# One 512-column product for both parts of x where the weights are stationary, and a later place for scores and transposes in an encoder kernel

## The chip, the cores and the metric

The kernel runs on one core of one Trainium2 chip. The metric is the device time of one execution in microseconds. The traces come from the hardware profiler, one execution each. The engines are named as in the profile: PE (TensorE; PEld are its weight loads), DVE (VectorE), ACT (ScalarE), POOL (GpSimd) and SP (SyncE, which issues the loads).

## The reference

A two-layer encoder over 256 tokens of width 1024. Each layer is a gated feed-forward block, a mixer block and a second feed-forward block, each followed by a layer norm:

```python
for l in range(2):
    x = layer_norm(ALPHA * x + 0.5 * (silu(x @ wg1[l]) * (x @ wu1[l])) @ wd1[l])      # d_ff = 2816
    u, gb, gc, h, q, k, v = jnp.split(x @ w_in[l], [256, 512, 768, 1024, 1536, 2048], axis=-1)
    y_a = pool_mixer(u)                          # window means minus the token, a small product
    y_b = gb * conv3(gc * h)                     # depthwise, width 3
    y_c = neighbourhood_attention(q, k, v)       # 8 heads of 64, 4 x 64 grid, bias, softmax
    x = layer_norm(ALPHA * x + jnp.concatenate([y_a, y_b, y_c], -1) @ w_out[l])
    x = layer_norm(ALPHA * x + 0.5 * (silu(x @ wg2[l]) * (x @ wu2[l])) @ wd2[l])
```

All of it is in fp32. The kernel gets fp32 accuracy from the faster fp32r format: x and the weights are each split into a high part (hi, the value rounded to fp32r) and a low part (lo, the rest), and a product is hi·hi + hi·lo + lo·hi.

## The kernel before

**Weights.** They are loaded in units of 128 x 1024 values on SP's queue. ACT makes the high part of a unit (`upper`, L218, `whi`), DVE the low part (`lower`, L223, `wlo`). 11 pairs are kept ahead.

**Three forms of product.** `x_stat` (L345 to L347) holds a tile of x and streams 512 columns of weights; `r_stat` (L370 to L372) does the same for the down and output products. `w_stat` (L349) is the other way round: a 128 x 128 chunk of weights is stationary and the 256 tokens of x stream, so that the result comes out with features on the partitions. It is used where that layout is wanted: for the last 256 columns of gate and up in each feed-forward block, and in the mixer for q0, k0, q1, k1, gc and h, 256 columns each: 20 products in all. A product has two column tiles of 128 (`ft`), each the sum over 8 chunks of three matmuls: high weights by high x (L358), high weights by low x (L359), low weights by high x (L360). Both column tiles go side by side into one PSUM bank, which one consumer reads as 512 columns.

**Order.** The order on each engine is that in which the code emits it, steered by a paced clock (`Pacer`). `pc.step(us)` moves that clock on by the PE time of the work just emitted; `pc.at(delay, tag, fn)` puts a piece of work off until the clock has passed now plus delay; `pc.need(tag)` emits what is still put off. Steps also emit the splits of the weights that have landed. A step is a quarter of a w_stat product, so what is put off comes out at quarters.

**The mixer.** v, u and gb come first. Then `qk(0)` makes q0 and k0 for the first four heads and puts off their attention, two heads (a pair, `first` and `second`) at a time; `qk(1)` does it for the other four; then come gc and h. Attention of a pair has four pieces: `scores` (PE L799, DVE's bias and maximum L808 and L810, ACT's exponentials L813), `normalise` (DVE L823 and L825), `transposed` (PE L834, ACT's copies `PT` L839) and `weighted` (PE L848, then yT by ACT L861 and DVE L862). The delays are A_S and A_STEP for the scores, then A_NORM, A_TR and A_PV from piece to piece. `conv_mixer` (L771) is a chain on DVE from z = gc·h (L894) over the taps (L775, L777) to the product with gb (L778), then ACT's cast (L780) and DVE's rest (L781). At the end the output product runs over eight chunks, first those of y_a, then of attention, then of the convolution.

**Banks.** PSUM has eight banks. Four ("acc") hold the long sums and the scores, four ("mm") rotate among all other products and transposes; a new one takes the bank that was released first, and PE waits until its last reader is through.

The x parts are two tiles (`xhi`, `xlo`), each written once per block by `transpose_x` (L319).

Of the kernel before, what the change touches and what calls it, by code (L numbers as in the profile page):

```python
# [9 lines left out]
F32 = mybir.dt.float32  # L10
F32R = mybir.dt.float32r
AF = mybir.ActivationFunctionType
ALU = mybir.AluOpType
# [3 lines left out]
P = 128  # L17
SEQ = 256
NT = SEQ // P
D = 1024  # L20
KC = D // P
# [3 lines left out]
HD = 64  # L25
# [8 lines left out]
QB = GRID // 2  # L34
# [17 lines left out]
H_TR = 4.1  # L52
U_TR = 2.6
POOL_AT = 22.0
A_S = 1.5
A_STEP = 0.8
A_NORM = 3.6
A_TR = 2.2
A_PV = 1.4
BIAS_AT = A_S + A_STEP + A_NORM + A_TR + 0.6  # L60

# [1 line left out]
LOWER = 0.9  # L63

MM512 = 0.218
MM256 = 0.1095


class Pacer:
# [75 lines left out]
def encoder_kernel(  # L145
# [7 lines left out]
    PE, ACT, DVE, POOL, SP = nc.tensor, nc.scalar, nc.vector, nc.gpsimd, nc.sync  # L153
# [5 lines left out]
    xp = ctx.enter_context(tc.tile_pool(name="xp", bufs=1))  # L159
    tp = ctx.enter_context(tc.tile_pool(name="tp", bufs=5))  # L160
# [9 lines left out]
    def nm(s):  # L170
        counter[0] += 1
        return f"{s}_{counter[0]}"

    def f32(t):
        return t.bitcast(F32)
# [4 lines left out]
    def mirrored(v):  # L180

        dims = [list(d) for d in v.ap]
        step, n = dims[-1]
        dims[-1] = [-step, n]
        return bass.AP(tensor=v.tensor, offset=v.offset + (n - 1) * step, ap=dims)
# [4 lines left out]
    def bank(tag="mm"):  # L190
        pool = ps_mm if tag == "mm" else ps_acc
        return pool.tile([P, 512], F32, tag=tag, name=nm(tag))
# [66 lines left out]
    def behind(q):  # L259

        return [[4 * q - 4, 4 * q - 3], [4 * q - 2, 4 * q - 1]]
# [20 lines left out]
    pc = Pacer(units, fetch, upper, lower)  # L282
# [29 lines left out]
    POOL.memset(half_t, -0.5)  # L312

    def new_xT():
        hi = xp.tile([P, KC, SEQ], F32R, tag="xhi", name=nm("xhi"))
        lo = xp.tile([P, KC, SEQ], F32R, tag="xlo", name=nm("xlo"))
        return hi, lo

    def transpose_x(t, k0, n, xT, tag="mm"):  # L319
        ts = slice(t * P, (t + 1) * P)  # L320
# [25 lines left out]
            PE.matmul(ps, xT[1][:, kc, ts], hi[:, j, :], start=False, stop=False)  # L346
            PE.matmul(ps, xT[0][:, kc, ts], lo[:, j, :], start=False, stop=(kc == KC - 1))  # L347

    def w_stat(ps, key, xT):  # L349

        for ft in range(2):
            c = slice(ft * P, (ft + 1) * P)
            for i in range(2):
                hi, lo = pc.get((*key, i))
                for j in range(4):
                    kc = i * 4 + j
                    o = ps[:, ft * SEQ : (ft + 1) * SEQ]
                    PE.matmul(o, hi[:, j, c], xT[0][:, kc, :], start=(kc == 0), stop=False)  # L358
                    PE.matmul(o, hi[:, j, c], xT[1][:, kc, :], start=False, stop=False)  # L359
                    PE.matmul(o, lo[:, j, c], xT[0][:, kc, :], start=False, stop=(kc == KC - 1))  # L360
                if ft == 1:
                    pc.free((*key, i))
                if ft == 0 or i == 0:
                    pc.step(12 * MM256)

    def r_stat(ps, key, act, t, n, first, last, c=slice(0, 512), again=False):

# [33 lines left out]
    def finish(keys, act, acc, last_key, next_gb, store, stop):  # L401

        nT = None if store else new_xT()
        wide = slice(0, 512)
        pieces = {(t, n): [(wide, acc[t][n])] for t in range(NT) for n in range(2)}
# [49 lines left out]
    def new_h():  # L455
        return hp.tile([P, 2, 2, SEQ], F32R, tag="h", name=nm("hT"))

    def silu(gate):
        sg = tp.tile([P, 512], F32, tag="t", name=nm("sg"))
        ACT.activation(sg, gate, AF.Silu)  # L460
        return sg

    def gated(up, sg):
        hf = tp.tile([P, 512], F32, tag="t", name=nm("hf"))
        DVE.scalar_tensor_tensor(hf, up, 0.5, sg, ALU.mult, ALU.mult)
        return hf

    def ffn(key, xT, next_gb, stop, store=False):
# [19 lines left out]
        if key == (0, 0):  # L488
# [8 lines left out]
            for h in range(2):  # L497
                transpose_x(h, 0, 2, xT, "acc")
                keep_warm(1)
                raw, hi, lo = [f[:, h] for f in first]  # L500
# [7 lines left out]
            for k in (gk, uk):  # L508
                ps = [bank() for _ in range(NT)]
# [14 lines left out]
        else:  # L524
            for t in range(NT):
                pc.need(f"x{t}")
                gate = bank()
                x_stat(gate, gk, 512, t, xT, t == 1)
                sg = silu(gate)
                pc.step(6 * MM512)  # L530
                up = bank()
# [14 lines left out]
        def down(fs):  # L546
            for f in fs:
                k = (*key, "d", f)
                for t in range(NT):
                    for n in range(2):  # L550
                        if acc[t][n] is None:
                            acc[t][n] = bank("acc")

                        ends = store and (f, t, n) == (behind(GROUPS[-1])[1][-1], 1, 1)
                        r_stat(acc[t][n], k, act(k), t, n, f == 0, ends)
                    if t == 1:
                        pc.free(k)
                    pc.step(6 * MM512)
# [13 lines left out]
        for q in GROUPS:  # L572
# [9 lines left out]
                gated_transposed(q, t, sgs[t], ups[t])  # L582
            pc.step(6 * MM512)
            down(behind(q)[1])
        gate = bank()
        w_stat(gate, (*key, "g", "last"), xT)
        sg = silu(gate)
        pc.step(12 * MM256)
        pc.need("h")
        up = bank()  # L590
        w_stat(up, (*key, "u", "last"), xT)
        hT = hts[NPAIR - 1] = new_h()
        hf = gated(up, sg).rearrange("p (a b) -> p a b", a=2)
        ACT.copy(hT[:, 0], hf)
        DVE.tensor_tensor(hT[:, 1], hf, f32(hT[:, 0]), ALU.subtract)
        pc.step(12 * MM256)
        keys = [(*key, "d", f) for f in range(2 * (NPAIR - TAIL), NCH)]
        return finish(keys, act, acc, keys[-1], next_gb, store, stop)

# [98 lines left out]
    def mixers(l, xT, next_gb, stop):  # L698
        key = (l, 1)
# [63 lines left out]
            pc.at(U_TR, "u", spread)  # L763
            pc.step(6 * MM512)

        def proj(name):
            ps = bank()
            w_stat(ps, (*key, name), xT)
            return ps.rearrange("p (a b) -> p a b", a=2)

        def conv_mixer(z):  # L771
            s = ap_.tile([P, 2, SEQ], F32, tag="a", name=nm("cs"))
            for j in range(2):
                tap = [cw[:, (l * 3 + k) * 2 + j : (l * 3 + k) * 2 + j + 1] for k in range(3)]
                DVE.tensor_scalar(s[:, j, :], z[:, j, 0:SEQ], tap[0], None, ALU.mult)  # L775
                for k in (1, 2):
                    DVE.scalar_tensor_tensor(s[:, j, :], z[:, j, k : k + SEQ], tap[k], s[:, j, :], ALU.mult, ALU.add)  # L777
            DVE.tensor_tensor(s, s, GB, ALU.mult)  # L778
            new_y(1)
            ACT.copy(ys[1][:, 0], s)  # L780
            DVE.tensor_tensor(ys[1][:, 1], s, f32(ys[1][:, 0]), ALU.subtract)  # L781

        def attention(j, qT, kT, q):
# [6 lines left out]
            def inner(z, b):  # L790
                return z[:, b, :, b * KOFF : b * KOFF + KW]
# [28 lines left out]
            def normalise():  # L820
                for e in range(2):
                    sm = st["sm"][e]
                    DVE.reciprocal(sm, sm)  # L823
                    for b in range(2):
                        DVE.tensor_scalar(inner(new[e], b), inner(new[e], b), sm[:, b : b + 1], None, ALU.mult)  # L825
                pc.at(A_TR, tag, transposed)

# [36 lines left out]
            return scores  # L864

        def qk(q):
            pq = proj(f"q{q}")
            qT = hp.tile([P, 2, 2, P], F32, tag="qk", bufs=4, name=nm("qT"))
            for j in range(2):
                for b in range(2):  # L870
                    src = mirrored(pq[:, j, :].rearrange("p (r c) -> p r c", c=GRID)[:, :, b * QB : (b + 1) * QB])
                    ACT.mul(qT[:, j, b, :].rearrange("p (r c) -> p r c", c=QB), src, HD ** -0.5)
            pc.step(12 * MM256)
            pk = proj(f"k{q}")
            kT = hp.tile([P, 2, SEQ], F32, tag="qk", bufs=4, name=nm("kT"))
            ACT.copy(kT, pk)
            first = attention(0, qT, kT, q)
            second = attention(1, qT, kT, q)
            pc.at(A_S, f"a{q}", first)
            pc.at(A_S + A_STEP, f"a{q}", second)  # L880
            pc.step(12 * MM256)

        qk(0)
        pc.at(BIAS_AT, "bias1", lambda: biases.update({1: add_mask(rv1)}))
        qk(1)
        p_ = proj("gc")
        gc = ap_.tile([P, 2, SEQ], F32, tag="a", name=nm("gc"))
        ACT.copy(gc, p_)
        pc.step(12 * MM256)
        p_ = proj("h")  # L890
        z = ap_.tile([P, 2, SEQ + 2], F32, tag="a", name=nm("z"))
        POOL.memset(z[:, :, 0:1], 0.0)
        POOL.memset(z[:, :, SEQ + 1 :], 0.0)
        DVE.tensor_tensor(z[:, :, 1 : SEQ + 1], p_, gc, ALU.mult)  # L894
        conv_mixer(z)
        pc.step(12 * MM256)

        acc = [[None, None], [None, None]]

# [19 lines left out]
    pc.at(GB_AT, "gb", lambda: load_gb(0, 0))  # L919
    pc.at(GB_AT + 4, "setup", setup)  # L920
    xT = new_xT()
    order = [(l, i) for l in range(DEPTH) for i in range(3)] + [None]
    for i, (l, part) in enumerate(order[:-1]):
        nxt = order[i + 1]
        if part == 1:
            xT = mixers(l, xT, nxt, starts[i + 1] + 8)
        else:
            xT = ffn((l, part), xT, nxt, starts[i + 1] + 8, store=nxt is None)
# [30 lines left out]
```

## Time and profile before

| | |
|---|---|
| median of 3 runs | 949.89 us (949.8 to 949.92) |
| the profiled execution, and its span in the trace | 950.0 us, 948.2 us |
| busy share of the span: PE, PEld, DVE, ACT, POOL | 99%, 84%, 61%, 47%, 6% |
| PE matmuls by line: x_stat 3 x 704, w_stat 3 x 320, r_stat 3 x 352 | 392, 287 and 393 ns each for the first of the three lines |
| mean clock granted to PE | 0.998 of full speed |

In the page, a group's row has the line, the engine and operation, output <- inputs, the shapes and the count, then the busy time, the mean duration of one in ns, the idle time of the engine before it and what ended that. In the timeline the first column is the start and the second the duration, and a bracket says how long the engine was idle before and what released it. A matmul's duration overlaps the next one's, so the time it takes of the array is read from start to start.

### The profile page before, as it was taken

Reading aid. Unit: us, or ns where it says so; the run is one execution under the profiler, and the core shown is the slowest. Engines: PE = TensorE matmul, PEld = TensorE weight load, DVE = VectorE, ACT = ScalarE, POOL = GpSimd, SP = SyncE. Lnnn points to the kernel's source line nnn. Section 1 sums busy time; section 2 is a strip of 40 time slices with the busy share of each in tenths; the row PEclk is TensorE's granted clock in tenths of the full one; section 3 lists DMA queues with packets and bytes.
Section 4 is the critical chain, followed back from the end, with each engine's and each line's share of the span. In section 5 each row is a group of like instructions: output and inputs, shape, how many; then the busy total and the mean of one; then the engine's idle time right before and its main releaser. Section 6 shows DMA issues by size and latency. Waiting matters only on the chain.

```text
span 948.2 us, 12782 instructions
## 1 busy us (share of the span) xinstructions
PE 938.1 (99%) x4819; PEld 793.6 (84%) x4819; DVE 577.5 (61%) x723; ACT 447.0 (47%) x622; POOL 60.9 (6%) x106
## 2 busy tenths in 40 slices
PE   9999999999999999999999999999999999999996
PEld 6888888989988888888888888888898888888895
DVE  5854454686777654555675555557777875554535
ACT  6644444346735544443444444444565554444420
POOL 4000100005100000000000001000060000000000
PEclk9999999999999999999999999999999999999999
DMA  9877486447444866655458657654645457656401
GB/s 324 304 256 226 107 297 194 133 139 239 153 137 156 270 233 185 196 182 163 144 172 264 233 157 224 212 173 143 201 151 174 156 188 249 217 189 194 161 1 45
DMA packets 96590, 178.81 MB, mean 189 GB/s; under 512 B 14784, under 2 KB 35856, under 8 KB 96528
## 3 DMA queue, kind: packets, MB, share of 16 engines
q1 hardware_dynamic: 96240, 177.60, 58.4%
q8 instruction: 38, 0.62, 0.3%
q10 hardware_dynamic: 288, 0.39, 0.1%
q14 instruction: 24, 0.20, 0.1%
HBM read 176.84 MB, written 1.13 MB: 188 GB/s over the span
## 4 chain that ended last, share of the span: by engine, by line
PE 99%; DVE 1%; ACT 0%; issue 0%; DVEq 0%
PE mm L347 17%; PE mm L345 17%; PE mm L346 17%; PE acc L370 10%; PE acc L371 10%; PE acc L372 10%; PE mm L358 4%; PE mm L360 4%; PE mm L359 4%; PE mm L477 2%; PE mm L323 1%; PE mm L834 1%; PE mm L848 1%; PE acc L799 1%; PE acc L309 0%; PE mm L757 0%
## 5 line engine op out<-in xcount | busy, mean ns | idle before, releaser
L223 DVE TENSOR_TENSOR wlo<-raw,whi 128x1024 fp32r<-128x1024 f32 (+1 forms) x322 | 389.8, 1234 | 209.8 <-ACT whi L218 209.5
L218 ACT CAST whi<-raw 128x1024 fp32r<-128x1024 f32 (+1 forms) x322 | 332.5, 1044 | 319.5 <-PE mm L346 150.6
L345 PE MATMUL mm<-whi,xhi 128*128 128x512 f32 x704 | 275.8, 392 | 0.3 <-ACT whi L218 0.3
L347 PE MATMUL mm<-wlo,xhi 128*128 128x512 f32 x704 | 274.4, 390 | 0.2 <-DVE wlo L223 0.2
L346 PE MATMUL mm<-whi,xlo 128*128 128x512 f32 x704 | 274.0, 389 | 0.0
L347 PEld LDWEIGHTS mm<-wlo,xhi 128*128 128x128 f32 x704 | 132.1, 188 | 28.8 <-DVE wlo L223 1.0
L345 PEld LDWEIGHTS mm<-whi,xhi 128*128 128x128 f32 x704 | 132.3, 188 | 28.4 <-ACT whi L218 1.1
L346 PEld LDWEIGHTS mm<-whi,xlo 128*128 128x128 f32 x704 | 132.3, 188 | 26.9
L370 PE MATMUL acc<-whi,hT 128*128 128x512 f32 (+1 forms) x352 | 138.4, 393 | 0.0
L371 PE MATMUL acc<-whi,hT 128*128 128x512 f32 (+1 forms) x352 | 136.5, 388 | 0.0
L372 PE MATMUL acc<-wlo,hT 128*128 128x512 f32 (+1 forms) x352 | 136.5, 388 | 0.0
L358 PE MATMUL mm<-xhi,whi 128*128 128x256 f32 x320 | 92.0, 287 | 0.0
L360 PE MATMUL mm<-xhi,wlo 128*128 128x256 f32 x320 | 90.5, 283 | 0.0
L359 PE MATMUL mm<-xlo,whi 128*128 128x256 f32 x320 | 90.5, 283 | 0.0
L372 PEld LDWEIGHTS acc<-wlo,hT 128*128 128x128 f32 x352 | 66.1, 188 | 13.6
L482 DVE TENSOR_TENSOR hT<-mm,hT 128x256 fp32r<-128x256 f32 x80 | 32.4, 423 | 73.1 <-ACT hT L481 73.1
L370 PEld LDWEIGHTS acc<-whi,hT 128*128 128x128 f32 x352 | 66.2, 188 | 12.7
L371 PEld LDWEIGHTS acc<-whi,hT 128*128 128x128 f32 x352 | 66.2, 188 | 12.6
L358 PEld LDWEIGHTS mm<-xhi,whi 128*128 128x128 f32 x320 | 61.3, 192 | 1.7 <-issue 1.5
L359 PEld LDWEIGHTS mm<-xlo,whi 128*128 128x128 f32 x320 | 61.3, 192 | 0.3
L360 PEld LDWEIGHTS mm<-xhi,wlo 128*128 128x128 f32 x320 | 61.3, 192 | 0.0
L393 POOL TENSOR_TENSOR rs<-rs,half_t 128x1 f32<-128x1 f32 x12 | 11.7, 979 | 637.5 <-DVE rs L392 637.5
(110 smaller groups left out, 584.2 us busy)
## 6 DMA issues: line engine op xcount, KB each, us to landing
raw<-in_ffn_w_up_dram SPq DMA_DIRECT2D x88, 512.0 KB, 4.6
raw<-in_ffn_w_down_dram SPq DMA_DIRECT2D x88, 512.0 KB, 4.4
raw<-in_ffn_w_gate_dram SPq DMA_DIRECT2D x87, 512.0 KB, 4.6
raw<-in_w_in_dram SPq DMA_DIRECT2D x40, 512.0 KB, 4.1
raw<-in_w_out_dram SPq DMA_DIRECT2D x16, 512.0 KB, 4.9
lng<-in_ln_g_dram SPq DMA_DIRECT2D x6, 512.0 KB, 5.4
lnb<-in_ln_b_dram SPq DMA_DIRECT2D x6, 512.0 KB, 6.5
rbias<-tab SPq DMA_DIRECT2D x16, 96.0 KB, 4.3
```

The lines of the kernel that those rows point to most:

```text
L218: ACT.copy(u, r)
L223: DVE.tensor_tensor(d, r, f32(u), ALU.subtract)
L345: PE.matmul(ps, xT[0][:, kc, ts], hi[:, j, :], start=(kc == 0), stop=False)
L346: PE.matmul(ps, xT[1][:, kc, ts], hi[:, j, :], start=False, stop=False)
L347: PE.matmul(ps, xT[0][:, kc, ts], lo[:, j, :], start=False, stop=(kc == KC - 1))
L358: PE.matmul(o, hi[:, j, c], xT[0][:, kc, :], start=(kc == 0), stop=False)
L359: PE.matmul(o, hi[:, j, c], xT[1][:, kc, :], start=False, stop=False)
L360: PE.matmul(o, lo[:, j, c], xT[0][:, kc, :], start=False, stop=(kc == KC - 1))
L370: PE.matmul(ps, act[0][:, ts], hi[:, n, c], start=first, stop=False, skip_group_check=again)
L371: PE.matmul(ps, act[1][:, ts], hi[:, n, c], start=False, stop=False, skip_group_check=again)
L372: PE.matmul(ps, act[0][:, ts], lo[:, n, c], start=False, stop=last, skip_group_check=again)
L482: DVE.tensor_tensor(h[:, 1, :, ts], src, f32(h[:, 0, :, ts]), ALU.subtract)
```

## The change

`x`'s two parts lie in one tile, per chunk of 128 features the 256 high and then the 256 low values. In `w_stat` one matmul with the high weights streams all 512 columns into a bank: hi·hi into the first half, hi·lo into the second. The matmul with the low weights streams the 256 high values and adds into the first half. The two halves are added at the end of each column tile: ACT copies the second half to SBUF, DVE adds the first half from PSUM. So a column tile has a bank of its own, and the consumers read SBUF. The factors that they applied before (1/8 for q, 0.5 for up) go into that sum. In the schedule, A_S is 2.1 instead of 1.5 and A_TR 3.0 instead of 2.2, and a quarter of a product counts as 4 x 0.341 us instead of 12 x 0.1095.

```diff
-A_S = 1.5
+A_S = 2.1
...
-A_TR = 2.2
+A_TR = 3.0
...
-MM256 = 0.1095
+MM768 = 0.341
...
     def new_xT():
-        hi = xp.tile([P, KC, SEQ], F32R, tag="xhi", name=nm("xhi"))
-        lo = xp.tile([P, KC, SEQ], F32R, tag="xlo", name=nm("xlo"))
-        return hi, lo
+        both = xp.tile([P, KC, 2, SEQ], F32R, tag="xT", name=nm("xT"))
+        return both[:, :, 0], both[:, :, 1], both.rearrange("p k i s -> p k (i s)")
...
-    def w_stat(ps, key, xT):
+    def w_stat(key, xT, out, scale=1.0):
         for ft in range(2):
             c = slice(ft * P, (ft + 1) * P)
+            ps = bank()
             for i in range(2):
                 hi, lo = pc.get((*key, i))
                 for j in range(4):
                     kc = i * 4 + j
-                    o = ps[:, ft * SEQ : (ft + 1) * SEQ]
-                    PE.matmul(o, hi[:, j, c], xT[0][:, kc, :], start=(kc == 0), stop=False)
-                    PE.matmul(o, hi[:, j, c], xT[1][:, kc, :], start=False, stop=False)
-                    PE.matmul(o, lo[:, j, c], xT[0][:, kc, :], start=False, stop=(kc == KC - 1))
+                    PE.matmul(ps, hi[:, j, c], xT[2][:, kc], start=(kc == 0), stop=False, skip_group_check=True)
+                    PE.matmul(
+                        ps[:, 0:SEQ], lo[:, j, c], xT[0][:, kc],
+                        start=False, stop=(kc == KC - 1), skip_group_check=True,
+                    )
                 if ft == 1:
                     pc.free((*key, i))
+                if i == 1:
+                    o = out[:, ft]
+                    ACT.activation(o, ps[:, SEQ:], AF.Copy, scale=scale)
+                    DVE.scalar_tensor_tensor(o, ps[:, 0:SEQ], scale, o, ALU.mult, ALU.add)
                 if ft == 0 or i == 0:
-                    pc.step(12 * MM256)
+                    pc.step(4 * MM768)
...
-        gate = bank()
-        w_stat(gate, (*key, "g", "last"), xT)
-        sg = silu(gate)
-        pc.step(12 * MM256)
+        sg = tp.tile([P, 2, SEQ], F32, tag="t", name=nm("sg"))
+        w_stat((*key, "g", "last"), xT, sg)
+        ACT.activation(sg, sg, AF.Silu)
+        pc.step(4 * MM768)
         pc.need("h")
-        up = bank()
-        w_stat(up, (*key, "u", "last"), xT)
+        hf = tp.tile([P, 2, SEQ], F32, tag="t", name=nm("hf"))
+        w_stat((*key, "u", "last"), xT, hf, 0.5)
         hT = hts[NPAIR - 1] = new_h()
-        hf = gated(up, sg).rearrange("p (a b) -> p a b", a=2)
+        DVE.tensor_tensor(hf, hf, sg, ALU.mult)
...
-            pk = proj(f"k{q}")
             kT = hp.tile([P, 2, SEQ], F32, tag="qk", bufs=4, name=nm("kT"))
-            ACT.copy(kT, pk)
+            w_stat((*key, f"k{q}"), xT, kT)
...
-        p_ = proj("gc")
         gc = ap_.tile([P, 2, SEQ], F32, tag="a", name=nm("gc"))
-        ACT.copy(gc, p_)
-        pc.step(12 * MM256)
-        p_ = proj("h")
+        w_stat((*key, "gc"), xT, gc)
+        pc.step(4 * MM768)
+        h = tp.tile([P, 2, SEQ], F32, tag="t", name=nm("h"))
+        w_stat((*key, "h"), xT, h)
...
-        DVE.tensor_tensor(z[:, :, 1 : SEQ + 1], p_, gc, ALU.mult)
+        DVE.tensor_tensor(z[:, :, 1 : SEQ + 1], h, gc, ALU.mult)
```

The order moves at two places that the prediction speaks of, both in the mixer of the first layer (the second has the same). The first is ACT at the end of the mixer. PT are the copies of transposed probabilities, four for the second head group; yT from cs is the cast at the end of the convolution; yT from mm is attention's result; gc and h are the evictions of these products. Before:

```order
L839 COPY PT_2546<-mm_2541 128x512
L839 COPY PT_2553<-mm_2548 128x512
L839 COPY PT_2560<-mm_2555 128x512
L839 COPY PT_2567<-mm_2562 128x512
L218 CAST whi_2581<-raw_2267 128x1024
L780 CAST yT_2608<-cs_2600 128x512
L861 CAST yT_2616<-mm_2611 128x4x32 x2
L861 CAST yT_2616<-mm_2621 128x4x32 x2
```

Now:

```order
L367 ACTIVATE h_2427<-mm_2428 128x256
L840 COPY PT_2470<-mm_2465 128x512
L840 COPY PT_2477<-mm_2472 128x512
L218 CAST whi_2479<-raw_2205 128x1024
L367 ACTIVATE h_2427<-mm_2456 128x256
L781 CAST yT_2504<-cs_2496 128x512
L840 COPY PT_2512<-mm_2507 128x512
L840 COPY PT_2519<-mm_2514 128x512
```

The second pair's two copies have moved from in front of the convolution's cast to behind it. On PE their transposes now stand behind h's product, and the weighted sum that reads them stands inside the output product, behind its first twelve matmuls.

The second place is DVE between the scaling of the first head group and gc's product. pz are probabilities, sm their sums, wlo low parts of weights, kT the keys of the second head group. Before:

```order
L825 TENSOR_SCALAR pz_737<-pz_737,sm_2197 128x4x40 x2
L823 RECIPROCAL sm_2204<-sm_2204 128x2
L825 TENSOR_SCALAR pz_739<-pz_739,sm_2204 128x4x40 x2
L223 TENSOR_TENSOR wlo_2235<-raw_2000,whi_2234 128x1024
L223 TENSOR_TENSOR wlo_2270<-raw_2039,whi_2269 128x1024
```

Now:

```order
L223 TENSOR_TENSOR wlo_2181<-raw_1976,whi_2180 128x1024
L824 RECIPROCAL sm_2161<-sm_2161 128x2
L826 TENSOR_SCALAR pz_736<-pz_736,sm_2161 128x4x40 x2
L824 RECIPROCAL sm_2168<-sm_2168 128x2
L826 TENSOR_SCALAR pz_738<-pz_738,sm_2168 128x4x40 x2
L223 TENSOR_TENSOR wlo_2208<-raw_2012,whi_2207 128x1024
L368 SCALAR_TENSOR_TENSOR kT_2210<-mm_2211,kT_2210 128x256
L368 SCALAR_TENSOR_TENSOR kT_2210<-mm_2239,kT_2210 128x256
```

The two adds of the keys are new; they stand behind a weight split, and the second pair's scaling stands behind another. Before, the bank of these keys was freed by one ACT copy.

More of the change, by code (lines that the diff above doesn't have):

```diff
@@ L764, in mixers @@
             pc.step(6 * MM512)
[L766 to L769, printed above, removed]
         def conv_mixer(z):
@@ L866, in qk @@
         def qk(q):
-            pq = proj(f"q{q}")
+            pq = tp.tile([P, 2, SEQ], F32, tag="t", name=nm("q"))
+            w_stat((*key, f"q{q}"), xT, pq, HD ** -0.5)
             qT = hp.tile([P, 2, 2, P], F32, tag="qk", bufs=4, name=nm("qT"))
@@ L871, in qk @@
                     src = mirrored(pq[:, j, :].rearrange("p (r c) -> p r c", c=GRID)[:, :, b * QB : (b + 1) * QB])
-                    ACT.mul(qT[:, j, b, :].rearrange("p (r c) -> p r c", c=QB), src, HD ** -0.5)
-            pc.step(12 * MM256)
-            pk = proj(f"k{q}")
+                    ACT.copy(qT[:, j, b, :].rearrange("p (r c) -> p r c", c=QB), src)
+            pc.step(4 * MM768)
             kT = hp.tile([P, 2, SEQ], F32, tag="qk", bufs=4, name=nm("kT"))
-            ACT.copy(kT, pk)
+            w_stat((*key, f"k{q}"), xT, kT)
             first = attention(0, qT, kT, q)
@@ L880, in qk @@
             pc.at(A_S + A_STEP, f"a{q}", second)
-            pc.step(12 * MM256)
+            pc.step(4 * MM768)
         qk(0)
@@ L885, in mixers @@
         qk(1)
-        p_ = proj("gc")
         gc = ap_.tile([P, 2, SEQ], F32, tag="a", name=nm("gc"))
-        ACT.copy(gc, p_)
-        pc.step(12 * MM256)
-        p_ = proj("h")
+        w_stat((*key, "gc"), xT, gc)
+        pc.step(4 * MM768)
+        h = tp.tile([P, 2, SEQ], F32, tag="t", name=nm("h"))
+        w_stat((*key, "h"), xT, h)
         z = ap_.tile([P, 2, SEQ + 2], F32, tag="a", name=nm("z"))
@@ L893, in mixers @@
         POOL.memset(z[:, :, SEQ + 1 :], 0.0)
-        DVE.tensor_tensor(z[:, :, 1 : SEQ + 1], p_, gc, ALU.mult)
+        DVE.tensor_tensor(z[:, :, 1 : SEQ + 1], h, gc, ALU.mult)
         conv_mixer(z)
-        pc.step(12 * MM256)
+        pc.step(4 * MM768)
         acc = [[None, None], [None, None]]
```

## The prediction

> **What bounds the kernel now.** I read the head of the page and the chain of work that ended last first.
>
> ```profile
> span 948.2 us, 12782 instructions
> PE 938.1 (99%) x4819; PEld 793.6 (84%) x4819; DVE 577.5 (61%) x723; ACT 447.0 (47%) x622; POOL 60.9 (6%) x106
> PE 99%; DVE 1%; ACT 0%; issue 0%; DVEq 0%
> ```
>
> The chain is PE from end to end. So two things count: how much array time PE's instructions take, and where PE has to wait. ACT and DVE have room on average, but each runs its instructions in order, and a wait arises where an eviction stands behind something late.
>
> Next the timeline of PE, for the price of one matmul. A row's second column is a pipelined duration; the price is the distance between starts. For 512 columns I take one whole feed-forward group from the chain, for 256 columns a run inside one product.
>
> ```profile
> 376.62 0.87 PE mm L477 x8
> 410.15 0.87 PE mm L477 x8
> ```
>
> ```profile
> 252.92 0.28 PE L359 MATMUL mm<-xlo,whi 128*128 128x256 f32 x1
> ...
> 258.43 0.28 PE L360 MATMUL mm<-xhi,wlo 128*128 128x256 f32 x1
> 258.55 1.93 PE L834 MATMUL mm<-ident,pz 128*128 128x128 f32 x16
> 260.24 0.36 PE L358 MATMUL mm<-xhi,whi 128*128 128x256 f32 x1
> 260.44 0.28 PE L359 MATMUL mm<-xlo,whi 128*128 128x256 f32 x1
> ```
>
> From 376.62 to 410.15 lie 33.53 us: 8 transposes (0.87 us), a restart (0.08, as from 260.24 to 260.44 against the usual 0.12) and, by the code, 48 gate, 48 up and 48 down products: (33.53 - 0.95) / 144 = 0.2262 us per 512 columns. From 252.92 to 258.43 lie 46 steps: 0.1198 us per 256 columns. The 256 extra columns cost 0.1064 us, so every matmul carries about 0.0134 us that does not depend on its width.
>
> The third thing to see is where PE waits today. The timeline shows one place, once per mixer: the sixteen transposes of the first head group's probabilities.
>
> ```profile
> 240.30 2.52 PE L834 MATMUL mm<-ident,pz 128*128 128x128 f32 x16
> ```
>
> Against 1.93 us for the same sixteen at 258.55 that is 0.6 us, waiting for DVE's scaling. Two mixers: 1.2 us in all.
>
> **The matmuls.** The change leaves out one matmul per weight chunk: 20 products of 2 column tiles of 8 chunks are 320. Three of 256 cost 0.3594 us, one of 512 and one of 256 0.2262 + 0.1198 = 0.3460. A change of width costs nothing of its own in these rows:
>
> ```profile
> 177.71 0.28 PE L360 MATMUL mm<-xhi,wlo 128*128 128x256 f32 x1
> 177.83 0.40 PE L370 MATMUL acc<-whi,hT 128*128 128x512 f32 x1
> 178.06 0.40 PE L371 MATMUL acc<-whi,hT 128*128 128x512 f32 x1
> ```
>
> A 256 in front of a 512 takes 0.12, the 512 takes 0.23. So the saving is 320 x 0.0134 = 4.3 us; by these single rows (0.35 instead of 0.3594) 3.0 us, the other end.
>
> The Trainium skill, page "TensorE: Matmul & The Clock Gate", section "Back-to-back issue gap", puts the isolated gap at N/2.4 + 2.5 ns, a fixed part of 2.5 ns. By it the 320 would be worth 0.8 us as an estimate; the trace's fixed part is five times that, so the rows decide.
>
> **Restarts.** PE's change between fp32 groups and the products costs something:
>
> ```profile
> 248.91 0.28 PE L360 MATMUL mm<-xhi,wlo 128*128 128x256 f32 x1
> 249.12 1.36 PE L799 MATMUL acc<-kT,qT 64*128 64x160 f32 x16
> 250.41 0.39 PE L358 MATMUL mm<-xhi,whi 128*128 128x256 f32 x1
> 250.63 0.28 PE L359 MATMUL mm<-xlo,whi 128*128 128x256 f32 x1
> ```
>
> 0.21 and 0.22 stand where 0.12 is the pitch: 0.19 us per group of scores or weighted sums, 0.08 after transposes. The pairs of heads now come apart: one more fp32 group and two more of transposes per mixer, 0.35 us, so +0.7 us.
>
> **The new evictions.** Each column tile now needs an ACT copy and a DVE add of 256 columns, where one instruction took 512 (or the consumer read PSUM). The nearest rows:
>
> ```profile
> L482 DVE TENSOR_TENSOR hT<-mm,hT 128x256 fp32r<-128x256 f32 x80 | 32.4, 423 | 73.1 <-ACT hT L481 73.1
> L481 ACT CAST hT<-mm 128x256 fp32r<-128x256 f32 x80 | 28.2, 374 | 43.5 <-PE mm L477 22.9 <-DVE hT L482 20.6
> ```
>
> 0.37 and 0.42 us; I take 0.45 for the add with its hand-over. The feed-forward's last gate and up hide them: from the end of up to the last hT it is 0.37 + 0.45 and three 512-wide operations of 0.6 to 0.7, about 3 us, and PE has 18 products of 512 (4.07 us) before it reads that hT. No cost there; without that cover it would be 3 us four times. In the mixer the queues are fuller. I add up ACT's and DVE's rows, in the built order, at four places, with these prices:
>
> ```profile
> 241.51 0.16 DVE L823 RECIPROCAL sm<-sm 128x2 f32<-128x2 f32 x1
> 241.71 0.52 DVE L825 TENSOR_SCALAR pz<-pz,sm 128x160 f32<-128x160 f32 x2
> 242.14 2.35 DVE L223 TENSOR_TENSOR wlo<-raw,whi 128x1024 fp32r<-128x1024 f32 x2
> ```
>
> ```profile
> 250.04 0.49 DVE L808 TENSOR_TENSOR Sb<-acc,bias 128x320 f32<-128x320 f32 x1
> 250.56 0.49 DVE L810 TENSOR_REDUCE mx<-Sb 128x2 f32<-128x320 f32 x1
> ```
>
> ```profile
> L813 ACT ACTIVATE pz<-Sb,mx 128x160 f32<-128x160 f32 x32 | 13.4, 420 | 3.8 <-DVE mx L810 3.7
> ```
>
> ```profile
> 233.66 1.28 ACT L813 ACT_TABLE_LOAD   x1 [1.73 <-DVE mx L810]
> ```
>
> A head's scaling takes DVE 0.63 us (241.51 to 242.14), a weight split 1.12 back to back, a head's bias and maximum 0.95; an exponential takes ACT 0.41.
>
> *First transposes (q0's first pair).* PE, from the end of k0's product: seven quarters of a product at 4 x 0.346 = 1.38 and two groups of scores at 0.8 make 11.3; it wants the second head 0.4 later. In the first layer: scores done at 2.1, first maximum 3.1, table load to 4.4, four exponentials to 6.1, eviction of q1's first tile 6.5, its add 7.0; behind that on DVE the second pair's maxima, 7.9 and 8.8; exponentials to 9.7, a weight cast to 10.6, q1's second eviction 11.0, its add 11.4, two heads' scaling 12.7. PE waits 1.0. In the second layer the table is loaded early, all ends 1.2 sooner, at 11.5, and PE does not wait. So 1.0 and 0 instead of 0.6 and 0.6: -0.2 us. Ends: both gone (-1.2), or GpSimd's bias sums in DVE's way (+1.8), as here:
>
> ```profile
> L825 DVE TENSOR_SCALAR pz<-pz,sm x32: 284/302/1491, 238.7 to 725.1; 128x160 f32<-128x160 f32 x32
> ```
>
> *The bank of gc.* gc's first tile takes the bank of k1's first tile, free once DVE has added that. From the add of q1's second tile on, DVE has 0.35 + 1.26 (two heads) + 1.12 + 1.26 + 1.12 + 0.45 = 5.6 us. In the second layer this runs from 9.8 to 15.4; PE arrives at 11.3 + 0.93 + 1.38 + 0.93 = 14.5. Wait 0.9 there, 1.1 in the first: +2.0 us. Ends 0 and 3.0.
>
> *Transposes of q1's first pair.* Their scaling stands behind gc's second add, that behind ACT's eviction, that behind this:
>
> ```profile
> 254.75 0.81 ACT L736 ACTIVATE ya<-mm,cw 128x256 f32<-128x256 f32 x2
> ...
> 257.06 0.57 ACT L888 COPY gc<-mm 128x512 f32<-128x512 f32 x1
> ```
>
> From gc's start: the exponentials end at 10.9, ya, its cast and a weight cast take 2.3 (254.75 to 257.06), eviction 13.5, add 14.0, two heads 15.2. PE has seven quarters (9.7), two groups of weighted sums and scores (1.7 each) and the pooling product (0.7): 13.9, the second head at 14.3. Wait 1.0 us a layer, +1.9 in both. Ends 0 and 3.0.
>
> *Weighted sum of q1's second pair.* The dearest. Today:
>
> ```profile
> 259.19 2.05 ACT L839 COPY PT<-mm 128x512 f32<-128x512 f32 x4 [0.59 <-PE mm L834]
> ...
> 267.72 0.62 ACT L780 CAST yT<-cs 128x512 fp32r<-128x512 f32 x1 [4.83 <-DVE cs L778]
> ```
>
> ```profile
> 263.28 1.95 PE L848 MATMUL mm<-PT,v 128*64 128x256 f32 x16
> 265.16 0.50 PE L370 MATMUL acc<-whi,yT 128*128 128x512 f32 x1
> ```
>
> ```profile
> 263.39 0.69 DVE L894 TENSOR_TENSOR z<-mm,gc 128x512 f32<-128x512 f32 x1 [1.68 <-PE mm L360]
> ...
> 266.99 0.69 DVE L778 TENSOR_TENSOR cs<-cs,GB 128x512 f32<-128x512 f32 x1
> ```
>
> ACT stands idle for 4.83 us in front of the convolution's cast, until DVE's chain from z (263.39) to cs (267.68) is through; all four copies of transposed probabilities (PT) were done before. In the changed order two of the four stand behind that cast, and PE's last weighted sum reads them. Let H be the end of h's product. PE then has transposes (0.93), six products (1.36), the other weighted sum (half of 1.88, and 0.19), six products (1.36), a restart (0.09): it arrives at H + 4.9. DVE, from the end of the scaling that PE waited for (H - 1.9), still has a split, two heads, a split and two adds: 1.12 + 1.26 + 1.12 + 0.8, so z starts at H + 2.3. Then 4.29 to cs, the cast 0.62, two copies 1.1: the second lands at H + 8.3. PE uses it one slot (0.235) into the sum: a wait of 3.2 us. Were DVE's queue empty, z would start at H + 1.0 (copy and add) and the wait would be 1.9. I take 3.2, nearest to the built order: +6.3 us in two layers, ends 3.8 and 7.4 (half a split more each).
>
> **The sum.** -4.3 + 0.7 - 0.2 + 2.0 + 1.9 + 6.3 = +6.4 us. The profiled execution took 950.0 us (its span 948.2); that is 956.4, and 956.3 against the median of 949.89.
>
> **The rivals.**
> - *The waits shrink to what no queue hides:* only the convolution's own path stays (3.8), every other wait goes. -4.3 + 0.7 - 1.2 + 3.8 = -1.0, 948.9 us. For it: ACT is busy for 47% of the span. Against: the built order puts splits in front of the adds. 0.09.
> - *Faster:* PE waits nowhere, and the later emission takes away the 0.6 us per mixer. -4.3 + 0.7 - 1.2 = -4.8, 945.1 us. It decides if the PT copies land before H + 4.9, so if z to cs takes under 2.2 us even with an empty queue, against 4.29 in the rows. 0.09, for what I misread of the order.
> - *More waiting:* GpSimd holds DVE, and each wait goes to its upper end: -3.0 + 0.7 + 1.8 + 3.0 + 3.0 + 7.4 = +12.9, 962.8 us. 0.08.
> - *The fixed part belongs to the weight load and stays,* the 512 product waiting for its weights behind a 256 one: the saving goes and the time is 956.3 + 4.3 = 960.6. Against: the 0.12 at 177.71. 0.04. The page's 2.5 ns would come near it, 959.8.
>
> **How the numbers follow.** A measurement of this kernel can tell about 0.2%, 1.9 us, from no change. The forecast has 0.70. Slower: forecast, more waiting and the lost saving, 0.82; same: the shrunk waits, 0.09; faster 0.09. The range, 950.5 to 960.5, holds the forecast with two of its middle waits at either end, or with the last one at its lower end and one more gone (956.3 - 2.5 - 2.0 = 951.8); it leaves out the first two rivals, 0.18 together, and part of the third.
>
> **What would show it.** Right: 320 matmuls fewer; chunks 0.346 us apart in the products; the convolution's cast on ACT with two PT copies directly behind, and PE idle about 3 us before the last weighted sum in each mixer, put down to ACT's PT; idles of about 1 us before gc and before q1's transposes. Wrong: no idle at that sum, or chunks 0.357 us apart, or a time under 950.5.

## The result, and the profile after

The changed kernel takes 962.05 us (median of 4 runs, 959.98 to 962.8) against 949.9 us before (949.8 to 949.95, 4 runs): a ratio of 1.0124, 95% interval 1.0111 to 1.0136. It is slower, as forecast, but by 12.1 us where 6.4 were forecast, and outside the range. The profiled execution took 962.8 us. The head of its page and the chain:

```profile
span 961.0 us, 12207 instructions
PE 943.8 (98%) x4499; PEld 778.2 (81%) x4499; DVE 588.1 (61%) x763; ACT 457.6 (48%) x656; POOL 56.6 (6%) x106
PE 91%; DVE 5%; ACT 3%; issue 1%; DVEq 0%; ACTq 0%
```

The 320 matmuls are gone (4499 instead of 4819), and the chain now leaves PE for DVE and ACT. Where, the sum of PE's waits in the changed kernel says (the columns are the total, how often, and the longest):

```profile
PE mm L849 <- ACT PT L840: 5.5, 2, 2.7
PE mm L358 <- DVE kT L368: 1.8, 2, 0.9
...
PE mm L835 <- ACT qT L874: 0.9, 1, 0.9
```

The wait that the forecast called the dearest stands on top, once per mixer: the last weighted sum, for ACT's copy of the transposed probabilities. How much it cost a whole mixer is read from the eight transposes of x that open it to the eight that open the block behind it. First layer, PE's timeline of before and then of after:

```profile
203.27 1.03 PE L323 MATMUL mm<-ident,x 128*128 128x128 f32 x8
...
296.19 1.03 PE L323 MATMUL mm<-ident,x 128*128 128x128 f32 x8
```

```profile
202.96 1.03 PE L322 MATMUL mm<-ident,x 128*128 128x128 f32 x8
...
303.29 1.03 PE L322 MATMUL mm<-ident,x 128*128 128x128 f32 x8
```

The mixer grew from 92.92 to 100.33 us. In the second layer the same rows give 92.92 and 100.30 (669.27 to 762.19, and 676.00 to 776.30). That is +14.8 us for both. The feed-forward blocks give back about 0.2 us each, and the program's last stretch 1.1 us more, to which the end of the section on the forecast comes back.

The place of the long wait, in the timeline of after, DVE's chain, ACT and PE together:

```profile
266.69 0.69 DVE L895 TENSOR_TENSOR z<-h,gc 128x512 f32<-128x512 f32 x1
...
269.06 0.40 PE L378 MATMUL acc<-wlo,yT 128*128 128x512 f32 x1
...
270.30 0.69 DVE L779 TENSOR_TENSOR cs<-cs,GB 128x512 f32<-128x512 f32 x1
271.03 0.62 ACT L781 CAST yT<-cs 128x512 fp32r<-128x512 f32 x1 [6.10 <-DVE cs L779]
271.55 1.06 ACT L840 COPY PT<-mm 128x512 f32<-128x512 f32 x2
...
272.18 2.45 PE L849 MATMUL mm<-PT,v 128*64 128x256 f32 x8 [2.73 <-ACT PT L840]
...
274.56 0.80 PE L376 MATMUL acc<-whi,yT 128*128 128x512 f32 x1
275.16 0.57 PE L377 MATMUL acc<-whi,yT 128*128 128x512 f32 x1
```

This is the picture of the forecast almost to the tenth: ACT idles 6.10 us in front of the convolution's cast, while the copies of two heads' finished transposes wait behind that cast in ACT's own row. But the rows after it were not foreseen. The eight matmuls of the sum take 2.38 us (272.18 to 274.56), and the first product behind them 0.60 instead of 0.23. The answer of the windows (PE busy comes first, the granted clock is the third column from the end) names the reason. First layer, then second:

```profile
270.00:272.00 2.00, 0.00 (x0) 0.00 (x0) 1.28 (x3) 0.97 (x2) 0.00 (x0) 1.00 0.00 0
272.00:274.00 2.00, 1.82 (x7) 1.09 (x8) 1.75 (x3) 1.73 (x4) 0.00 (x0) 0.53 0.00 0
274.00:276.00 2.00, 2.00 (x7) 1.21 (x5) 1.67 (x4) 0.53 (x2) 0.00 (x0) 0.62 0.59 141
```

```profile
742.00:744.00 2.00, 0.08 (x1) 0.08 (x2) 1.28 (x3) 1.23 (x3) 0.00 (x0) 0.79 0.00 0
...
748.00:750.00 2.00, 2.00 (x6) 1.54 (x6) 1.27 (x2) 0.99 (x2) 0.00 (x0) 0.50 0.72 182
```

Behind the idle stretch PE runs at half clock: for about 3.4 us in the first layer ((1 - 0.53) x 2 / 0.5 + (1 - 0.62) x 2 / 0.5) and 6.8 us in the second ((1 - 0.79) x 2 / 0.5, and 6 us at 0.50 from 744 to 750). A wait that was priced at its own length had a second bill behind it.

### The profile page after: what moved, and what is told of

Read it like the earlier page. It is cut to its first block, busy times and chain, and to the rows that moved or that the text cites. A ratio compares the mean times of both kernels' runs of the same rounds, so it can differ in the third digit from the quotient of the medians.

```text
span 961.0 us, 12207 instructions
## 1 busy us (share of the span) xinstructions
PE 943.8 (98%) x4499; PEld 778.2 (81%) x4499; DVE 588.1 (61%) x763; ACT 457.6 (48%) x656; POOL 56.6 (6%) x106
## 4 chain that ended last, share of the span: by engine, by line
PE 91%; DVE 5%; ACT 3%; issue 1%; DVEq 0%; ACTq 0%
PE mm L346 17%; PE mm L344 17%; PE mm L345 17%; PE acc L376 10%; PE acc L377 10%; PE acc L378 10%; PE mm L358 5%; PE mm L359 2%; PE mm L483 2%; DVE wlo L223 1%; ACT pz L814 1%; PE mm L322 1%; DVE pz L826 1%; PE mm L849 1%; ACT whi L218 0%
## 5 line engine op out<-in xcount | busy, mean ns | idle before, releaser
L344 PE MATMUL mm<-whi,xT 128*128 128x512 f32 x704 | 275.8, 392 | 0.3 <-ACT whi L218 0.3
L346 PE MATMUL mm<-wlo,xT 128*128 128x512 f32 x704 | 274.4, 390 | 0.2 <-DVE wlo L223 0.2
L345 PE MATMUL mm<-whi,xT 128*128 128x512 f32 x704 | 274.0, 389 | 0.0
L346 PEld LDWEIGHTS mm<-wlo,xT 128*128 128x128 f32 x704 | 132.1, 188 | 28.9 <-DVE wlo L223 1.0
L344 PEld LDWEIGHTS mm<-whi,xT 128*128 128x128 f32 x704 | 132.3, 188 | 28.3 <-ACT whi L218 1.1
L345 PEld LDWEIGHTS mm<-whi,xT 128*128 128x128 f32 x704 | 132.3, 188 | 26.8
L358 PE MATMUL mm<-xT,whi 128*128 128x512 f32 x320 | 115.5, 403 | 1.8 <-DVE kT L368 1.8
L359 PE MATMUL mm<-xT,wlo 128*128 128x256 f32 x320 | 89.9, 281 | 0.0
L358 PEld LDWEIGHTS mm<-xT,whi 128*128 128x128 f32 x320 | 60.1, 188 | 17.4 <-DVE kT L368 2.3
L359 PEld LDWEIGHTS mm<-xT,wlo 128*128 128x128 f32 x320 | 60.5, 189 | 0.3
L487 ACT CAST hT<-mm 128x256 fp32r<-128x256 f32 x80 | 28.2, 374 | 43.6 <-PE mm L483 23.0
L466 ACT ACTIVATE sg<-mm 128x512 f32<-128x512 f32 x40 | 23.8, 598 | 30.1 <-PE mm L346 30.0
```

Of the source, the lines that this page charges most:

```text
L344: PE.matmul(ps, xT[0][:, kc, ts], hi[:, j, :], start=(kc == 0), stop=False)
L358: PE.matmul(ps, hi[:, j, c], xT[2][:, kc], start=(kc == 0), stop=False, skip_group_check=True)
L359: PE.matmul(ps[:, 0:SEQ], lo[:, j, c], xT[0][:, kc], start=False, stop=(kc == KC - 1), skip_group_check=True,)
L487: ACT.copy(h[:, 0, :, ts], src)
```

## Experiments

The theory after the trace: the later emission puts two PT copies behind the cast (wait), the idle time drops the clock (half clock), and the rest of the difference is smaller savings and dearer restarts than forecast. Rivals: the clock falls for a reason of its own; the new evictions, not the emission, make the wait. Each ratio is against the kernel before on the same chip; its medians there, 949.93 to 950.0 us, differ so little that the runs are also compared with each other.

**The cast behind the last weighted sum.**

```diff
-            ACT.copy(ys[1][:, 0], s)
-            DVE.tensor_tensor(ys[1][:, 1], s, f32(ys[1][:, 0]), ALU.subtract)
+
+            def cast():
+                ACT.copy(ys[1][:, 0], s)
+                DVE.tensor_tensor(ys[1][:, 1], s, f32(ys[1][:, 0]), ALU.subtract)
+
+            return cast
...
-        conv_mixer(z)
+        cast = conv_mixer(z)
...
         pc.need("a1")
+        cast()
```

> The convolution's cast and its remainder are emitted behind the last weighted sum; nothing else differs from the changed kernel. Theory (queue and clock): ACT's two PT copies no longer stand behind the cast, the wait of 2.7 us before the last weighted sum goes in both mixers, and with it the half clock that followed (worked out from the trace of after: 1.9 us in the first layer, 3.1 in the second). 962.1 - 2 x 2.8 - 5.0 = 951.5 us, granted clock 0.998 as before the change. Rival (the clock falls for a reason of its own, not for the idle time): only the waits go, 956.5 us, and the clock still falls to a half near 272 and 744 us. Rival (the wait moves): the copies are held by something else in ACT's row, 959 us or more.

Measured: 953.04 us, ratio 1.0033 [1.0021, 1.0044]. The weighted sum and what follows, PE's timeline of this run:

```profile
269.14 0.39 PE L378 MATMUL acc<-wlo,yT 128*128 128x512 f32 x1
269.46 1.08 PE L853 MATMUL mm<-PT,v 128*64 128x256 f32 x8
270.47 0.50 PE L376 MATMUL acc<-whi,yT 128*128 128x512 f32 x1
```

No wait, 1.01 us for the sum, full clock (0.998 or more in all six runs). One place in ACT's row made 9.0 of the 12.1 us. That gain is about 1.5 us smaller than expected; the next run says which half of the bill had been put too high.

**Filling the wait.** 24 products of 256 columns that nobody reads, written to the unused half of the weighted sum's bank; and in another run 12.

```diff
-                po = bank()[:, 0:SEQ].rearrange("p (b r c) -> p b r c", b=2, r=ROWS)
+                ps = bank()
+                if (q, j) == (1, 1):
+                    for _ in range(24):
+                        PE.matmul(
+                            ps[:, SEQ:], xT[0][:, 0, 0:P], xT[0][:, 0],
+                            start=True, stop=True, skip_group_check=True,
+                        )
+                po = ps[:, 0:SEQ].rearrange("p (b r c) -> p b r c", b=2, r=ROWS)
```

> Ahead of the last weighted sum PE gets 24 products of 256 columns whose results nobody reads (24 x 0.12 = 2.9 us), so that it is busy while it would wait. Everything else is the changed kernel. Theory (queue and clock): the wait stays as it is, only filled, and the half clock behind it does not come: 962.1 - 5.0 = 957.1 us, up to 957.6 if the filling outlasts the wait. Rival (the clock falls for a reason of its own): 962.1 to 962.6 us, clock at a half behind the weighted sum as in after.

> The changed kernel with 12 products of 256 columns ahead of the last weighted sum, whose results nobody reads (1.45 us), so that PE idles for about 1.4 us instead of 2.8. Theory (half clock only after more than about 2 us of idle): clock stays full and the time is that with 24 such products, 958.9 us. Rival (1.4 us are enough): 961 to 962 us, granted clock at a half behind the weighted sum.

Measured: 958.91 us with 24 and 958.99 with 12, ratios 1.0093 [1.0076, 1.0110] and 1.0094 [1.0080, 1.0108]. The same place in the timeline with 24, and the window behind it:

```profile
269.43 3.04 PE L848 MATMUL mm<-xT 128*128 128x256 f32 x24
272.40 1.49 PE L856 MATMUL mm<-PT,v 128*64 128x256 f32 x8
273.82 0.50 PE L376 MATMUL acc<-whi,yT 128*128 128x512 f32 x1
```

```profile
272.00:274.00 2.00, 2.00 (x13) 1.12 (x13) 1.74 (x3) 1.87 (x4) 0.00 (x0) 1.00 0.00 0
```

And with 12, where PE still idles 1.29 us:

```profile
272.25 1.56 PE L856 MATMUL mm<-PT,v 128*64 128x256 f32 x8 [1.29 <-ACT PT L840]
```

```profile
272.00:274.00 2.00, 1.75 (x9) 0.92 (x10) 1.74 (x3) 1.79 (x4) 0.00 (x0) 1.00 0.00 0
```

The sum still cannot start before 272.2, but the clock stays at 1.00 and the products behind it run at 0.23. All eight runs with such products have a mean clock of 0.997 to 0.999. So the idle time is what drops the clock, and the rival of a clock that falls by itself is out: a wait of 2.7 us brought the half clock, one of 1.3 us did not. The half clock is worth 962.05 - 958.91 = 3.1 us and the wait itself 958.91 - 953.04 = 5.9. I had read 5.0 for the clock off one execution; there the two mixers are 4.0 us longer than in the filled run, and the changed kernel alone scatters by 2.8 us (959.98 to 962.8), the filled ones by 0.4. The mean granted clock on record goes with that scatter: 0.996 in the run of 959.98 us, 0.994 at 961.8 and 962.3, 0.993 at 962.8. The difference of 0.003 over 960 us is about 2.9 us of full clock (an estimate; the clocks have three decimals), as much as the scatter. So it is most likely the half clock that lasts longer in one run than in another.

Narrow windows over the profiled execution of after show when the clock changes:

```profile
272.10:272.20 0.10, 0.02 (x1) 0.02 (x1) 0.10 (x1) 0.10 (x2) 0.00 (x0) 0.62 0.00 0
275.50:275.60 0.10, 0.10 (x2) 0.03 (x1) 0.10 (x1) 0.00 (x0) 0.00 (x0) 0.81 0.78 287
743.10:743.20 0.10, 0.00 (x0) 0.00 (x0) 0.00 (x0) 0.10 (x1) 0.00 (x0) 0.82 0.00 0
749.90:750.00 0.10, 0.10 (x2) 0.10 (x1) 0.10 (x1) 0.00 (x0) 0.00 (x0) 0.54 1.05 410
958.20:958.30 0.10, 0.00 (x0) 0.00 (x0) 0.00 (x0) 0.00 (x0) 0.00 (x0) 0.52 0.88 348
```

A mean between 0.5 and 1 says where in the window the change lies: down at 272.12, up at 275.54, down at 743.16, up at 749.99, and down at 958.20, behind the program's last matmul. Counted from the first, the others come 1, 138, 140 and 201 times 3.4133 us later (686.08 / 201). So all five changes of this execution lie on one grid with that step. The idle time of PE up to the fall was 2.7 us in the first layer, 2.0 us in the second and 4.2 us at the program's end, so it is no fixed time. How such a wait lies on the grid may decide whether the clock falls and for how many steps; that would explain the scatter, but no run moved the wait to test it.

**Emission times and products apart.** The merged products with the times of before, and the kernel before with the new times:

```diff
-A_S = 2.1
+A_S = 1.5
...
-A_TR = 3.0
+A_TR = 2.2
```

and in the kernel before

```diff
-A_S = 1.5
+A_S = 2.1
...
-A_TR = 2.2
+A_TR = 3.0
```

> The merged products with the emission times of before (scores 1.5, transposes 2.2). Theory (the later emission makes the dear wait): all four PT copies stand ahead of the convolution's cast, so no long wait and no half clock; products 2.0 us cheaper than before the change, the head groups stay together (no restarts more), the first transposes wait about 1.5 us per mixer instead of 0.6: 949.9 - 2.0 + 1.8 = 949.7 us, 948.5 to 951. Rival (the new evictions make it): 955 us or more, with a wait of over 2 us per mixer in front of a weighted sum or transposes.

> The kernel before with the new emission times alone (scores 2.1, transposes 3.0); products as before. Theory (the later emission makes the dear wait): two PT copies stand behind the cast here too; DVE has two adds of 0.4 less ahead of z, so PE waits about 2.0 us per mixer; with the half clock behind that (2.5 each, if 2 us of idle are enough) and head groups that come apart (about 1.0 per mixer), without the 0.6 at the first transposes: 949.9 + 2 x (2.0 + 2.5 + 1.0 - 0.6) = 959.7 us; without the half clock 954.7. Rival (the new evictions make it): 951 us or less.

Measured: old times 950.36 us, ratio 1.0004 [0.9995, 1.0014]; new times alone 952.34, ratio 1.0026 [1.0016, 1.0036]. The first came out as expected, without a row for a weighted sum among PE's waits: the merging alone does not make the dear wait. It is not free in the mixers, though, which are 1.4 and 0.8 us longer than before (94.34 and 93.76 us); the time comes out even because the feed-forward blocks and the program's end give that back. The second fell between its expectations: it was expected at 959.7 or, without half clock, 954.7, and its rival at 951 or less. Its timeline has the same figure, the two copies behind the cast, only milder:

```profile
267.07 0.62 ACT L780 CAST yT<-cs 128x512 fp32r<-128x512 f32 x1 [4.25 <-DVE cs L778]
...
267.60 1.07 ACT L839 COPY PT<-mm 128x512 f32<-128x512 f32 x2
...
268.23 1.56 PE L848 MATMUL mm<-PT,v 128*64 128x256 f32 x8 [0.73 <-ACT PT L839]
```

0.73 us of idle, no half clock (0.998 over the run). The emission alone thus costs 2.4 us and the merging alone 0.4; together they cost 12. Neither the theory nor its rival had that: the long wait needs both the later emission and the new evictions.

```profile
262.76 0.68 DVE L894 TENSOR_TENSOR z<-mm,gc 128x512 f32<-128x512 f32 x1
```

Here z starts 0.3 us behind the end of h's product (262.76 against 262.47), in after 2.4 (266.69 against 264.33): there the add of gc, what it held up, and the two adds of h stand ahead of z in DVE's row. Those 2.1 us carry the wait from 0.7 us to 2.7, and there the clock fell. This run also prices the groups that come apart: its mixers take 94.69 and 94.71 us (before 92.92); less the wait and the slowed sum (0.80 + 0.48), plus the 0.6 us at the first transposes that are gone, 1.1 us per mixer. Scores, for one, in this run:

```profile
231.75 0.81 PE L799 MATMUL acc<-kT,qT 64*128 64x160 f32 x8
232.50 0.39 PE L358 MATMUL mm<-xhi,whi 128*128 128x256 f32 x1
...
234.13 0.81 PE L799 MATMUL acc<-kT,qT 64*128 64x160 f32 x8
234.87 0.39 PE L358 MATMUL mm<-xhi,whi 128*128 128x256 f32 x1
```

Two halves take 0.75 and 0.74, the whole took 1.29 in the rows of before at 249.12: a split costs 0.2 us inside the group of scores, besides the two more changes of 0.1 that I had counted. Eight transposes take 0.80 us here (242.17 to 242.97) where sixteen took 1.69 (258.55 to 260.24 before): splitting those costs nothing that shows.

**Merging undone, all else kept.** On the kernel with the old times:

```diff
-                    PE.matmul(ps, hi[:, j, c], xT[2][:, kc], start=(kc == 0), stop=False, skip_group_check=True)
-                    PE.matmul(
-                        ps[:, 0:SEQ], lo[:, j, c], xT[0][:, kc],
-                        start=False, stop=(kc == KC - 1), skip_group_check=True,
-                    )
+                    a, b = ps[:, 0:SEQ], ps[:, SEQ:]
+                    PE.matmul(a, hi[:, j, c], xT[0][:, kc], start=(kc == 0), stop=False, skip_group_check=True)
+                    PE.matmul(b, hi[:, j, c], xT[1][:, kc], start=(kc == 0), stop=(kc == KC - 1), skip_group_check=True)
+                    PE.matmul(a, lo[:, j, c], xT[0][:, kc], start=False, stop=(kc == KC - 1), skip_group_check=True)
```

> The merged kernel with the old emission times, but each pair of products taken apart again into three of 256 columns (hi x hi and lo x hi into the two halves of the bank), so that evictions and order stay and only the merging goes. By the trace of after (0.3594 - 0.3532 = 0.0062 us for each of 320): 950.4 + 2.0 = 952.4 us. By the forecast (0.0134 each): 950.4 + 4.3 = 954.7 us.

This form does not compute the reference's sums (its result is off by 0.068; that two sums are started within one bank is the likely reason and was not tried), so only its time is used. Measured: 951.55 us, ratio 1.0016 [1.0008, 1.0025], so 1.2 us more than merged. The trace of after says 2.0:

```profile
234.58 0.28 PE L359 MATMUL mm<-xT,wlo 128*128 128x256 f32 x1
...
241.29 0.28 PE L359 MATMUL mm<-xT,wlo 128*128 128x256 f32 x1
```

19 pairs in 6.71 us are 0.3532 us each, against 0.3594 for three products: 0.0062 x 320 = 2.0. The difference is in the mixers: the two kernels' differ by 0.2 us per layer, not 0.6, since the merged one comes to the first transposes earlier and waits longer there (1.12 us instead of 0.70 in the first layer).

**Whole groups, later transposes; then the 512s first; then other banks.** Scores at 1.5, transposes at 3.0; second, in each quarter of a product the four matmuls of 512 columns before the four of 256; third, every second head's transposes in a bank of the accumulators:

```diff
-A_S = 2.1
+A_S = 1.5
...
                     PE.matmul(ps, hi[:, j, c], xT[2][:, kc], start=(kc == 0), stop=False, skip_group_check=True)
+                for j in range(4):
+                    kc = i * 4 + j
                     PE.matmul(
...
-                    tr = bank().rearrange("p (a b) -> p a b", a=2)
+                    tr = bank("acc" if e else "mm").rearrange("p (a b) -> p a b", a=2)
```

> The merged products, scores emitted at 1.5 as before the change (so the two pairs of heads stay together), transposes at 3.0 as after it. Theory (each cost has its own source): with the groups whole the 2.2 us of restarts that the run with the new times alone showed don't come; all four PT copies stand ahead of the convolution's cast, so no long wait and no half clock; the transposes come one quarter product (1.4 us) later than in the run with the old times, so its waits at them (1.8 and 1.2 us at the first, 0.6 and 0.6 at the second) go: 950.4 - 4.2 = 946.2 us, 945.5 to 947.5. Rival (a wait takes the place of each one removed, at a bank or at the weighted sums): 949 us or more.

> As the run with whole groups, but within a quarter product the four 512-column products come first and then the four of 256 columns. In after a pair of 512 and 256 took 0.3532 us instead of the 0.3460 of the forecast. Theory A (the 0.0072 is paid at each change from 256 to 512 columns): three in four go, 320 x 0.0072 x 0.75 = 1.7 us less than the run with whole groups. Theory B (it belongs to the 512-column product with these operands): the same time as that run, and the 512 still 0.237 apart.

> As the run with whole groups and the 512s first, but the transposes of every second head write to a bank of the accumulators instead of the products' four banks. In that run PE waits for the first PT copies to free a bank (rows of 0.24, 0.24 and 0.29 us put down to ACT's PT, one in the first layer put down to DVE's scaling of pz), and 0.31 for the add of kT. Theory (the banks cost it): the ACT rows go, 4 x 0.25 to 0.45 = 1.0 to 1.8 us less, 945.7 to 946.5 us. Rival (the scaling on DVE paces these transposes anyway): within 0.5 us of 947.5.

Measured: 948.24 us, ratio 0.9982 [0.9973, 0.9991]; with the 512s first 947.52, ratio 0.9974 [0.9964, 0.9985]; with the other banks as well 944.68, ratio 0.9944 [0.9930, 0.9957]. The first is faster than both kernels but short of its 946.2 and outside its 945.5 to 947.5, without reaching the rival's 949. PE's waits in the second run show what took the place:

```profile
PE mm L837 <- ACT PT L842: 0.8, 3, 0.3
PE mm L344 <- ACT whi L509: 0.6, 1, 0.6
PE mm L837 <- DVE pz L828: 0.5, 1, 0.5
...
PE mm L358 <- DVE kT L370: 0.3, 1, 0.3
```

Three of the waits at transposes are now for a copy that frees a bank, one (0.5) is still for the scaling. With the accumulators' banks all four rows are gone from the list, and the time fell by 2.8 us where 1.0 to 1.8 were expected: the four rows together are 2.2, and not all of them were waits for a bank, so the run does not say what each was worth. The order of the 512s gave 0.7 us, between theory A (1.7) and B (0):

```profile
223.82 1.09 PE L358 MATMUL mm<-xT,whi 128*128 128x512 f32 x4
224.75 0.64 PE L361 MATMUL mm<-xT,wlo 128*128 128x256 f32 x4
225.22 1.09 PE L358 MATMUL mm<-xT,whi 128*128 128x512 f32 x4
```

A quarter takes 1.40 us, 0.350 per pair: a part of the 0.0072 is paid at the change of width, and the larger part (0.004) stays. The four 512s take 0.93 us, 0.2325 each, against 0.2262 in a stream of their own.

## Why the forecast was right and wrong

Term by term, in us for the whole kernel:

| step | forecast | measured |
|---|---|---|
| 320 matmuls fewer | -4.3 | -2.0 (pitch in after) |
| groups that come apart | +0.7 | +2.2 (new times alone) |
| first transposes | -0.2 | +0.1 |
| bank of gc | +2.0 | +2.5 |
| transposes of q1's first pair | +1.9 | +0.6 |
| last weighted sum, the wait | +6.3 | +5.9 (cast moved against filled) |
| half clock behind it | none | +3.1 (filled against after) |

These make 12.4 against 12.1, nearer than they deserve: the 1.1 us at the program's end (below) are not in the table. With them the terms come to 11.3, and 0.8 us are not accounted for.

*The step that failed* is the price of the last weighted sum: "I take 3.2, nearest to the built order: +6.3 us in two layers, ends 3.8 and 7.4". The wait was sized well. DVE started z 2.4 us behind the end of h's product (forecast 2.3; its own terms, 4.3 - 1.9, give 2.4) and the second copy landed at 8.3 (forecast 8.3). But the ends 3.8 and 7.4 bound the wait and not its consequence. The Trainium skill, page "TensorE: Matmul & The Clock Gate", section "Part 1: The HAM clock gate (the "warmup" mystery)", says that the half clock is the default which an idle window of about 3.4 us brings back; here 2.0 and 2.7 us were enough, and the two stretches at half clock, 3.4 and 6.8 us, are one and two such windows. The measurement decides. The forecast's own upper end, 3.7 us a layer, was longer than that window, too. A wait of that size should have carried a second term: 3.4 us at half clock are 1.7 us per mixer (an estimate), 6.8 are 3.4. The runs showed 3.1 us for both mixers together. With the wait left in and the half clock taken out, the time was 958.91 us, inside the forecast's range.

*The matmuls* were mis-sized by half. The fixed part of 0.0134 us per matmul was measured in streams of one width. In the new stream a pair takes 0.3532 us instead of 0.3460, so that leaving out a matmul saves 0.0062; most of the difference is at the 512, which is followed after about 0.237 us, not 0.226. The rival of a fixed part that stays was half right; its evidence against, one 0.12 at a change of width, was a single row, and only of the 256.

*The restarts* were counted as changes of group, 0.35 per mixer, and the groups themselves taken as divisible. The scores are not (0.2 us for a split), and the whole came to 1.1.

*q1's transposes* were mis-sized by the same error from the other side. DVE was where the forecast had it: the first head's scaling done 14.7 us behind gc's start (247.06) and the second's 15.3 (forecast 14.6 and 15.2). DVE's timeline, where each head's scaling ends as the next row begins:

```profile
261.76 0.16 DVE L824 RECIPROCAL sm<-sm 128x2 f32<-128x2 f32 x1
...
262.39 1.22 DVE L223 TENSOR_TENSOR wlo<-raw,whi 128x1024 fp32r<-128x1024 f32 x1
```

And PE's row of the transposes:

```profile
261.82 1.26 PE L835 MATMUL mm<-ident,pz 128*128 128x128 f32 x8
```

PE came at 14.8 instead of 13.9, since its split groups, the pooling product and the pairs had all taken longer, and found its first head ready. What PE loses earlier it does not wait here, so restarts and this wait are in part one bill entered twice. Their sum (2.6 forecast, 2.8 measured) is nearly right though each is far off.

*The bank of gc* waited in both layers as argued:

```profile
245.01 1.13 PE L835 MATMUL mm<-ident,pz 128*128 128x128 f32 x8
247.06 0.50 PE L358 MATMUL mm<-xT,whi 128*128 128x512 f32 x1 [0.92 <-DVE kT L368]
```

2.05 us between these rows, where the same eight transposes take 0.79 when nothing waits, are 1.26 per mixer.

*The rival "more waiting"* has the measured time, 962.8 us, but not the mechanism. It had GpSimd hold DVE and every wait at its upper end. In after DVE's scaling, which once took 1491 ns before, never takes more than 305:

```profile
L826 DVE TENSOR_SCALAR pz<-pz,sm x32: 296/302/305, 242.0 to 736.3; 128x160 f32<-128x160 f32 x32
```

The last wait is 5.9 and not 7.4, q1's 0.6 and not 3.0. Its number is luck.

The direction, the place of the main wait and its mechanism held. The size failed by a consequence left out (+3.1 us) and by the matmuls (+2.3); the errors of the other terms (+1.5, +0.3, +0.5, -1.3 and -0.4) nearly cancel, which is luck too.

What stays open: in the profile before, the last row of DVE begins 5.5 us ahead of the end, in every other run of this study 4.4 to 4.5. It is the same work, and nothing here explains it. So every run is compared with a kernel whose end takes 1.1 us more: of the 1.7 and 2.4 us by which the runs with whole groups are faster than before, 1.1 come from there.

## What to carry to other kernels

An operation emitted on an in-order engine in front of work that is ready makes that work wait for the operation's whole input chain; look in the built order for what stands behind a late operand. A wait of PE of a few microseconds is priced with the stretch at half clock behind it, and two changes that each cost little can together make a long wait: test them apart. A small group of matmuls can have a price of its own, as the scores do, that is paid twice when it is split, and removing a matmul of a stream saves what the new stream's pitch says, not the old one's.

## What the runs showed of the hardware

- In both mixers of after PE was without work for 2.7 us, and the granted clock fell to a half 2.7 and 2.0 us behind the end of its last matmul (worked out from the windows). It stayed there 3.4 and 6.8 us. Behind the program's last matmul it fell only after 4.2 us. With waits of 1.3 us and 0.7 us it did not fall.
- The five changes of the clock in that execution lie whole multiples of 3.4133 us apart (1, 138, 140 and 201 steps from the first).
- In a stream that alternates 512 and 256 columns over changing weights a pair takes 0.3532 us; four and four take 0.350 per pair; streams of one width would make it 0.346.
- Eight matmuls of the scores (64 rows, 160 columns) take 0.75 us where sixteen take 1.29; eight transposes take 0.80 where sixteen take 1.69.
